# Layer 0 of a hybrid decoder: two feed-forward pairs by token halves and nine by seven products, with zero writes on GpSimd between its convolution additions

## The chip, the cores and the metric

The kernel runs on one core of one Trainium2 chip. The metric is the time of one execution on the device in microseconds (us), as the median of several runs. Where the text says TensorE (PE in the profile), VectorE (DVE), ScalarE (ACT), GpSimd (POOL) and SyncE (SP), it means the five engines of that core. PEld is TensorE's weight load, which overlaps its matmuls.

## The reference

The input is x, 512 tokens of 1024 channels in float32. Two layers follow, and a last RMSNorm. What matters here is layer 0:

```
h = x
# conformer convolution
a = glu(rmsnorm(h) @ w_pw1 + b_pw1)              # 1024 -> 2 x 1024
y = causal depthwise convolution of a, 31 taps, + b_dw
h = h + silu(layernorm(y)) @ w_pw2 + b_pw2       # the "second projection"
# feed-forward
gate, up = split(rmsnorm(h) @ w_up)              # 1024 -> 2 x 2816
h = h + (silu(gate) * up) @ w_down               # 2816 -> 1024
```

Layer 1 is a sliding-window attention over keys and values that are projected from h, and a second feed-forward part of the same shape.

## The kernel before, in words

**Matmuls.** Activations lie transposed: channels on the 128 partitions, tokens along the free dimension. A float32 number is split into two float32r parts, hi and lo, and a product is made of three matmuls, hi x hi, hi x lo and lo x hi (`mm3`, lines 376 to 382). ACT makes hi by a copy and DVE lo by a subtraction (`split_weights`, L294 and L297). The first weight chunks (`NATIVE`, line 133) aren't split and go through L378 in plain float32.

**The stream of weights.** A weight chunk is 128 x 1024 float32, 512 KB. `PLAN` (line 131) lists all chunks in the order in which TensorE uses them. At each use `advance` (lines 299 to 314) issues the loads of chunks up to nine ahead on SP's queue and splits up to three ahead.

**The feed-forward part of layer 0.** The 2816 hidden channels make 11 pairs of 256. `HALVES0` says how they are done.

- Pairs 0 to 3 are done by token halves. For tokens 0 to 255 each pair takes 96 up matmuls and 48 down matmuls of 256 columns (pair 0's up matmuls are native). For tokens 256 to 511 the activations' hi and lo lie side by side, so a hi weight takes both in one matmul of 512 columns and a lo weight one of 256 (`mm2`, L412 and L413). Their weights are loaded and split once for each half.
- Pairs 4 to 10 are done over all tokens by Strassen and Winograd's scheme: the up product is cut into 2 x 2 blocks and made by seven block products (`SEVEN`, line 56) in place of eight. A block product is 24 matmuls of 256 columns (`product`, line 801). Their down matmuls are 512 columns wide, 48 for a pair. Four of the weight blocks are sums (S1 to S4), four of the activation blocks too (T1 to T4).

The sums of weights are made in DRAM: a copy of one block (`copy_sums`), then a DMA from POOL's queue that adds another block to it (`prepare`, lines 277 to 291, L289). `share` says how many of them are issued at each use of a chunk: 0.45 until the products begin, 0.25 in them. The sums of activations are made by `Rows0.sums` (lines 1284 to 1308) on DVE, and split like weights.

**The order of the work.** The first half of the convolution comes first; then the second projection of the first half (`pw2`), the first half of pairs 0 to 3 (up, then down), and three block products A12 of pairs 4 to 6 (`FIRST`), which need the first half's tokens alone. While TensorE does this, the second half's convolution runs on the other engines. Then come the second projection of the second half, the second half of pairs 0 to 3, the remaining 46 block products, and the down matmuls of pairs 4 to 10.

**The convolution.** Of a channel tile's 31 taps, DVE does one part as multiply-adds (L1009). For the other part ACT multiplies (L1001) and POOL adds (L1002). `Half.background` (from line 1108) is a generator that emits the second half's convolution step by step, then its layer norm: squares, sums over channels on TensorE (L1058), scales (L1064 to L1085), their spread over the partitions by one matmul pair (L1089), and eight rows of z = silu(layernorm(y)), each split in hi and lo (L1101 to L1103, then `split`, L544 and L545). The second projection reads z.

**What sets the order.** Instructions are put in order at compile time: each engine takes what is ready, with the first emitted ahead, and `tc.issue_after(x)` forbids that an instruction be put ahead of x on x's engine. `job(generator, (g, n), ...)` says by which use g of a weight chunk how many steps n of a generator have been emitted (`pace`, lines 337 to 344). At run time each engine works through its own order and waits where an input isn't there.

## Time and profile before

| | |
|---|---|
| median of 3 runs | 1043.42 us (1043.19 to 1044.5) |
| the profiled execution | 1043.27 us |
| its span, first to last instruction | 1041.5 us |
| granted TensorE clock, mean | 0.997 |
| second projection of the second half starts | 243.47 us |
| block products of layer 0 start | 335.2 us |
| last convolution addition of POOL (L1002) ends | 208.7 us |

Positions are microseconds from the start of the span. In the profile a group of instructions is named by line, engine, operation and tiles, written as output<-inputs, with the shape and the number of instructions; behind the bar stand its busy time and the mean duration of one in ns, and behind the second bar the engine's idle time just before, with what ended it. A timeline row begins with the start and the duration in us. A matmul's duration overlaps that of its neighbours, so durations of matmuls can't be added.

### The profile page before, as it was taken

The numbers are of one execution on the slowest core, as the hardware profiler recorded it, in microseconds if no ns is written. First come the engines' busy times: TensorE is split into PE (matmuls) and PEld (weight loads), VectorE is DVE, ScalarE is ACT, GpSimd is POOL, SyncE is SP. The second block draws the span as 40 slices with busy tenths as digits, with TensorE's granted clock in tenths as the row PEclk, the third lists the DMA queues.
The fourth block names the chain that finished last, engine by engine and source line by source line (L and its number), as shares of the span: only waits on it lengthen the run. The fifth ranks groups of instructions, "written<-read, shape, count | busy, mean of one in ns | idle before, by whom it ended". The sixth has DMA issues, their size and how long they took to land.

```text
span 1041.5 us, 17709 instructions
## 1 busy us (share of the span) xinstructions
PE 1031.5 (99%) x6580; PEld 932.6 (90%) x6580; DVE 776.5 (75%) x1202; ACT 613.0 (59%) x1062; POOL 473.2 (45%) x569
## 2 busy tenths in 40 slices
PE   9999999999999999999999999999999999999996
PEld 8888889999988999998888877788989999898995
DVE  3999989978789777673536566678686877868777
ACT  3887798847776556552333565466655556554654
POOL 3999999930535233221214255405442334434134
PEclk9999999999999999999999999999999999999998
DMA  9999747999999988999969766955879988877742
GB/s 356 340 315 207 205 126 204 272 256 275 249 239 262 304 220 284 256 301 244 286 209 254 210 183 183 228 154 152 252 230 312 287 264 264 245 233 222 224 150 81
DMA packets 67282, 248.33 MB, mean 238 GB/s; under 512 B 7579, under 2 KB 13884, under 8 KB 66364
## 3 DMA queue, kind: packets, MB, share of 16 engines
q1 hardware_dynamic: 54236, 200.75, 55.9%
q0 software_dynamic: 12672, 46.14, 24.8%
q8 instruction: 51, 0.84, 0.3%
q10 hardware_dynamic: 288, 0.31, 0.1%
q14 instruction: 35, 0.29, 0.1%
HBM read 241.93 MB, written 97.52 MB: 326 GB/s over the span
## 4 chain that ended last, share of the span: by engine, by line
PE 98%; DMA 0%; DVE 0%; issue 0%; POOLq 0%; SPq 0%; POOL 0%; ACT 0%
PE bank L380 20%; PE bank L382 20%; PE bank L381 20%; PE bank L960 10%; PE bank L902 9%; PE bank L412 4%; PE bank L378 4%; PE bank L413 2%; PE bank L1441 1%; PE bank L1483 1%; PE bank L1470 1%; PE bank L1058 1%; PE bank L1607 1%; PE bank L948 1%; DMA both<-in_lead_dram 0%; PE bank L1562 0%
## 5 line engine op out<-in xcount | busy, mean ns | idle before, releaser
L297 DVE TENSOR_TENSOR wlo<-raw,whi 128x1024 fp32r<-128x1024 f32 x246 | 329.7, 1348 | 136.8 <-ACT whi L294 136.5
L294 ACT CAST whi<-raw 128x1024 fp32r<-128x1024 f32 x246 | 257.1, 1049 | 276.6 <-PE bank L381 194.1
L380 PE MATMUL bank<-quad,whi 128*128 128x256 f32 (+1 forms) x976 | 307.4, 317 | 0.0
L381 PE MATMUL bank<-quad,whi 128*128 128x256 f32 (+1 forms) x976 | 306.6, 315 | 0.0
L382 PE MATMUL bank<-quad,wlo 128*128 128x256 f32 (+1 forms) x976 | 305.7, 315 | 0.0
L380 PEld LDWEIGHTS bank<-quad,whi 128*128 128x128 f32 x976 | 185.5, 191 | 12.8 <-issue 1.6
L381 PEld LDWEIGHTS bank<-quad,whi 128*128 128x128 f32 x976 | 186.0, 191 | 11.9 <-issue 0.5
L382 PEld LDWEIGHTS bank<-quad,wlo 128*128 128x128 f32 x976 | 185.6, 191 | 11.8 <-issue 0.4
L853 POOL TENSOR_TENSOR up<-up 128x512 f32<-128x512 f32 x34 | 62.9, 1851 | 283.6 <-ACT up L850 283.6
L1002 POOL TENSOR_TENSOR pr<-pr,pr 128x256 f32<-128x256 f32 x208 | 155.4, 788 | 2.6 <-ACT pr L1001 2.5
L380 PE MATMUL bank<-rows,whi 128*128 128x256 f32 x488 | 138.0, 283 | 0.0
L381 PE MATMUL bank<-rows,whi 128*128 128x256 f32 x488 | 137.8, 282 | 0.0
L382 PE MATMUL bank<-rows,wlo 128*128 128x256 f32 x488 | 137.8, 282 | 0.0
L1009 DVE SCALAR_TENSOR_TENSOR bank<-apad,wdw,bank 128x256 f32<-128x256 f32 x248 | 112.4, 485 | 3.4
L1001 ACT ACTIVATE pr<-apad,wdw 128x256 f32<-128x256 f32 x208 | 98.3, 502 | 14.9 <-POOL pr L1002 13.1
L960 PE MATMUL bank<-quad,w 128*128 128x256 f32 x448 | 98.7, 380 | 0.0
L960 PEld LDWEIGHTS bank<-quad,w 128*128 128x128 f32 x448 | 84.9, 190 | 11.8 <-DVE bank L1009 0.2
L380 PEld LDWEIGHTS bank<-rows,whi 128*128 128x128 f32 x488 | 93.1, 191 | 0.3
L381 PEld LDWEIGHTS bank<-rows,whi 128*128 128x128 f32 x488 | 93.1, 191 | 0.3
L382 PEld LDWEIGHTS bank<-rows,wlo 128*128 128x128 f32 x488 | 93.0, 191 | 0.0
L491 POOL TENSOR_TENSOR tmp<-tmp,tmp 128x256 f32<-128x256 f32 (+1 forms) x28 | 26.8, 957 | 101.4 <-ACT tmp L487 96.2
L412 PE MATMUL bank<-quad,whi 128*128 128x512 f32 x168 | 59.7, 398 | 0.0
(230 smaller groups left out, 1635.9 us busy)
## 6 DMA issues: line engine op xcount, KB each, us to landing
raw<-in_W_dram SPq DMA_DIRECT2D x170, 512.0 KB, 5.7
raw<-sum SPq DMA_DIRECT2D x88, 512.0 KB, 5.4
sum<-in_W_dram SPq DMA_DIRECT2D x52, 512.0 KB, 6.2
sum<-in_W_dram POOLq DMA_DIRECT2D x44, 512.0 KB, 9.6
sum<-sum POOLq DMA_DIRECT2D x44, 512.0 KB, 8.5
sum<-in_W_dram SPq DMA_DIRECT2D x4, 3584.0 KB, 30.4
w<-in_W_dram SPq DMA_DIRECT2D x14, 512.0 KB, 8.6
sum<-in_W_dram SPq DMA_DIRECT2D x4, 1024.0 KB, 30.3
```

The costliest lines, as they stand in the source:

```text
L294: on_act = nc.scalar.copy(hi, src).ins
L297: latest[:] = [on_act, lo_engine[0].tensor_sub(lo, src, f32(hi)).ins]
L380: nc.tensor.matmul(out, w[0], x[0], start=start, stop=False, **kw)
L381: nc.tensor.matmul(out, w[0], x[1], start=False, stop=False, **kw)
L382: nc.tensor.matmul(out, w[1], x[0], start=False, stop=stop, **kw)
L412: nc.tensor.matmul(first[2], first[0], first[1], start=start, stop=False)
L853: pool_op(nc.gpsimd.tensor_mul(gate, gate, c[:, m, :, 1, :]))
L902: nc.tensor.matmul(out, x, w[:, ws], start=first and e == 0 and i == 0, stop=e == 1 and i == 2, skip_group_check=True)
L960: mm = nc.tensor.matmul(self.pb[:, w * W2:(w + 1) * W2], w1_of(ct, w, k), x[k] if x else xg[k][:, tok], start=k == 0, stop=k == KT - 1)
L1001: on_act = nc.scalar.mul(pr, a[:, j:j + W2], tap(j))
L1002: on_pool = pool_op(nc.gpsimd.tensor_add(pr, acc, pr))
L1009: on_dve = nc.vector.scalar_tensor_tensor(yt if i == nd - 1 else c, src, tap(i), c if i else self.shift, op0=ALU.mult, op1=ALU.add)
```

## The change

Pairs 0 and 1 are done by token halves, pairs 2 to 10 by seven products. The nine are done in two groups, pairs 2 to 6 and 7 to 10, each with its products and then its down matmuls (`GROUPS0`). All nine have their A12 product made ahead of the second half's second projection. The results wait in one quad and five tiles of their own (`keep`). The background job is paced at each half of such a product.

The sums over channels, the scales' small matmuls and the spread of the second half's layer norm are put behind the matmul that was emitted last (`stamp`). The steps of the jobs get new points, and `share` becomes 0.5 and 0.45. The pool of part 2 has four buffers in place of five, and odd pairs take their gate tile from the quads. After each of POOL's convolution additions of the second half, from the point where its job begins, and after each of its eight multiplications in the second half's down evacuation, POOL writes zeros to a tile of 128 x 64 (`let_go`).

```diff
-HALVES0 = ((0, 4), (4, 11))
-FIRST = (4, 5, 6)
+HALVES0 = ((0, 2), (2, 11))
+GROUPS0 = ((2, 7), (7, 11))
+FIRST = tuple(range(2, 11))
...
-    plan.extend(("up0", *step) for step in part2_products())
-    downs(*HALVES0[1])
+    for group in GROUPS0:
+        plan.extend(("up0", *step) for step in part2_products(group))
+        downs(*group)
...
-EARLY = (0, sum(u[0] == "up0" for u in UNITS), 9)
+EARLY = (0, 6, 9)
...
+    letting = []
+
     def pool_op(op):
         pooled[0] = op.ins
+        return op
+
+    def let_go(op):
+        if letting:
+            with tc.issue_after(op.ins):
+                pool_op(nc.gpsimd.memset(letting[0], 0.0))
         return op
...
-        nc.tensor.matmul(out, w[1], x[0], start=False, stop=stop, **kw)
+        stamp[0] = nc.tensor.matmul(out, w[1], x[0], start=False, stop=stop, **kw).ins
...
-                    pool_op(nc.gpsimd.tensor_mul(t, t, rs_bc))
+                    let_go(pool_op(nc.gpsimd.tensor_mul(t, t, rs_bc)))
...
-    def product(key, block, r, opens, closes=True):
+    def product(key, block, r, opens, between=None):
 
         w = [x.rearrange("p (a k c) -> p a k c", a=2, k=4) for x in get_seven(*key)]
         for which in range(2):
+            if which and between is not None:
+                between()
...
-                            on_pool = pool_op(nc.gpsimd.tensor_add(pr, acc, pr))
+                            on_pool = let_go(pool_op(nc.gpsimd.tensor_add(pr, acc, pr)))
...
                 for n, (_, f) in enumerate(due):
-                    f()
+                    with tc.issue_after(stamp[0]):
+                        f()
                     for _ in range((4, 1)[n]):
                         yield
-                self.scales_a()
+                with tc.issue_after(stamp[0]):
+                    self.scales_a()
                 yield
                 self.scales_b()
                 withheld.clear()
                 yield
                 yield
                 yield
-                self.spread()
+                with tc.issue_after(stamp[0]):
+                    self.spread()
                 yield from self.rows(True)
...
-        job(second, (base, 0), (base + 8, 19), (base + 13, 22), (base + 26, 40), (base + 30, 45), (base + 34, 50), (base + 35, h1.n_steps - early - 3))
+        letting.append(cpool.tile([P, 64], F32, tag="letting", name="letting"))
+        job(second, (base, 0), (base + 8, 19), (base + 13, 22), (base + 27, 39), (base + 33, 43), (base + 34, 44), (base + 35, 44),
+            (base + 36, 46), (base + 37, 48), (base + 38, 49), (base + 40, h1.n_steps - early))
...
-        preparing[0], share[0] = prepare(), 0.45
+        preparing[0], share[0] = prepare(), 0.5
...
-            product(("up0", pair, "A12"), [[x0["ffn0"][4 + k][e][:, HALF[0]] for k in range(4)] for e in range(2)], r, True)
+            product(("up0", pair, "A12"), [[x0["ffn0"][4 + k][e][:, HALF[0]] for k in range(4)] for e in range(2)], r, True, pace)
...
-    job(rows0.sums(), (base + 11, 0), (base + 19, 8), (base + 26, 14), (base + 32, 17))
+    job(rows0.sums(), (base + 10, 0), (base + 14, 8), (base + 18, 12), (base + 23, 14), (base + 27, 17))
     pw2(h1.z, n1)
     ffn_part(0, 0, x0["ffn0"], HALF[1], n1.rms, twin=True)
-    flush()
...
-    share[0] = 1 / 4
+    share[0] = 0.45
+    for group in GROUPS0:
...
+            if pair not in open_pairs:
+                if pair % 2:
+                    c = quads.tile([P, 2, 2, 2, 256], F32, tag="quad", name=uid("up"))
+                else:
+                    c = z0.tile([P, 2, 2, 2, 256], F32, tag="z0", name=uid("up"), bufs=4)
+                open_pairs[pair] = SevenPair("up0", pair, rows0, c, first.get(pair))
+            pace()
+            open_pairs[pair].take(a)
...
```

77 lines of the change are left out of this document (41 added, 36 removed).

## The prediction

> **What bounds the kernel now.** I read the page first: span, busy shares, and the chain of work that ended last.
>
> ```profile
> span 1041.5 us, 17709 instructions
> PE 1031.5 (99%) x6580; PEld 932.6 (90%) x6580; DVE 776.5 (75%) x1202; ACT 613.0 (59%) x1062; POOL 473.2 (45%) x569
> PE 98%; DMA 0%; DVE 0%; issue 0%; POOLq 0%; SPq 0%; POOL 0%; ACT 0%
> ```
>
> TensorE is never without work, and the chain consists of it: the time is the sum of matmul spacings, and no other engine makes it wait. So a change gains what it takes off TensorE's list, as long as no wait appears. A busy time of one matmul overlaps its neighbour's, so the price of one is taken from stretches that hold one form: length divided by count. The next view gives the busy time of each engine in such stretches (us and number of matmuls under PE; the last two columns are the share of time that the DMA engines were busy, and GB/s).
>
> ```profile
> core 0: us, PE busy (x) PEld busy (x) DVE busy (x) ACT busy (x) POOL busy (x), PEclk, DMA share, GB/s
> 234.74:243.47 8.73, 8.73 (x72) 8.49 (x71) 8.70 (x18) 6.09 (x11) 0.00 (x0) 1.00 1.05 268
> 266.81:312.69 45.88, 45.88 (x264) 40.01 (x263) 37.60 (x43) 33.23 (x58) 18.94 (x18) 1.00 0.96 258
> 312.69:335.21 22.52, 22.52 (x129) 19.59 (x128) 22.32 (x28) 14.13 (x21) 10.18 (x10) 1.00 0.93 270
> 335.22:464.08 128.86, 128.86 (x1082) 128.86 (x1080) 95.90 (x110) 72.34 (x94) 37.45 (x28) 1.00 0.92 267
> 477.90:543.18 65.28, 65.28 (x289) 54.05 (x288) 25.86 (x26) 20.34 (x26) 12.65 (x17) 1.00 0.88 258
> ```
>
> They are: the three early products (72 matmuls); the second half's up matmuls of four pairs; its down matmuls; 45 products; and 288 down matmuls over all 512 tokens. An edge can add one or two to a count. The clock is 1.00 throughout.
>
> **What leaves TensorE.** A pair done by token halves costs:
> - first half: 96 up and 48 down matmuls of 256 columns at 8.73/72 = 0.1213 us: 11.64 + 5.82 us;
> - second half: (45.88 - 0.6 for the six norm matmuls in it)/4 = 11.32 and 22.52/4 = 5.63 us.
>
> Together 34.41 us. By seven products it costs one early product of 8.73/3 = 2.91, six of 128.86/45 = 2.864, and 48 wide down matmuls of 65.28/288 = 0.2267: 2.91 + 17.18 + 10.88 = 30.97 us. Two pairs gain 2 x 3.44 = 6.88. Four more pairs have their A12 product moved to the early place, 0.05 each dearer: **6.7 us** net. Without a new wait the profiled execution (1043.27 us, its span plus 1.8; the median shown is 1043.42) becomes **1036.6 us**.
>
> **Weights.** A moved pair needs 9 chunks in place of 2 x 6, so six splits (ACT L294, DVE L297) go, beside TensorE's work: nothing gained directly. Eight more sums are copied and added by DMA, eight more additions issued on POOL's queue: hidden unless the DMA engines run short (a rival).
>
> **The first new wait: the second projection.** It needs z of the second half's convolution, which DVE, POOL and ACT make while TensorE works on the first half. Two pairs' up and down work (2 x 17.46 us) goes from ahead of it, six products (17.46 us) come, so TensorE arrives 17.46 us earlier than at 243.47: at 226.0. What z went through before:
>
> ```profile
> 172.17:234.73 62.56, 62.56 (x510) 61.93 (x509) 53.62 (x76) 40.16 (x68) 42.78 (x47) 1.00 0.96 264
> 215.92 0.87 DVE L1009 SCALAR_TENSOR_TENSOR y<-apad,wdw,bank 128x256 f32<-128x256 f32 x2
> 216.54 2.42 POOL L1013 TENSOR_TENSOR y<-y,pr 128x256 f32<-128x256 f32 x2 [7.84 <-DVE y L1009]
> 234.28 1.02 PE L1089 MATMUL bank<-tmp,ones_m 128*128 128x512 f32 x2
> 240.99 0.76 DVE L545 TENSOR_TENSOR quad<-tmp,quad 128x256 fp32r<-128x256 f32 x2
> 251.83 0.75 DVE L545 TENSOR_TENSOR quad<-tmp,quad 128x256 fp32r<-128x256 f32 x2
> ```
>
> The first row is the first half's split matmuls: 480 x 0.1213 = 58.2 us, and 4.3 for norms (0.6) and the convolution's sums and spread. The taps ended at 216.8, y at 218.9, the spread of the scales ran at 234.28, the first two rows of z stood at 241.8, two us ahead of need, and the last two at 252.6 (their chunk was due at 252.2). The order of the tail is now tied to the products: sums after the first half of the seventh, spread after the first half of the ninth.
>
> Do the taps end in time? The costs in 157.7:216.7, and of zero writes at the start:
>
> ```profile
> L297 DVE TENSOR_TENSOR wlo<-raw,whi 128x1024 fp32r<-128x1024 f32 x17 | 26.5, 1567 | 2.1 <-ACT whi L294 2.1
> L662 DVE TENSOR_TENSOR bank<-bank,tmp 128x512 f32<-128x512 f32 x4 | 2.7, 687 | 0.0
> L1002 POOL TENSOR_TENSOR pr<-pr,pr 128x256 f32<-128x256 f32 x66 | 57.4, 918 | 2.6 <-ACT pr L1001 2.5
> L937 POOL MEMSET apad<- 128x30 f32 x8 | 0.6, 121 | 0.0
> L462 POOL MEMSET ones_m<- 128x128 f32 x1 | 0.2, 205 | 0.0
> 206.84 1.86 POOL L1002 TENSOR_TENSOR pr<-pr,pr 128x256 f32<-128x256 f32 x2
> 186.51 3.08 POOL L1002 TENSOR_TENSOR pr<-pr,pr 128x256 f32<-128x256 f32 x4
> 187.24 3.45 DVE L297 TENSOR_TENSOR wlo<-raw,whi 128x1024 fp32r<-128x1024 f32 x1
> 214.79 1.22 DVE L297 TENSOR_TENSOR wlo<-raw,whi 128x1024 fp32r<-128x1024 f32 x1
> ```
>
> A split takes 1.22 us when POOL is quiet, and took 3.45 behind POOL's run of four additions. The 17 took 26.5 us, so 26.5 - 17 x 1.22 = 5.8 us were waiting. POOL's additions suffer too: 66 from 137 to 209 took 0.918 us on average. The zero writes, one after each addition, break the runs: DVE gains 0 to 5.8 us; I take half. Up to the end of the taps DVE further loses 1.5 splits (2.4 us), six of the twelve gate operations (4.1) and 2.1 idle, and gets eight down evacuations (5.5, which came later before). So they end 3.1 to 8.9 us earlier, at 208 to 214. POOL gets 66 writes of 64 columns, which no row shows. Rows of 30 and 128 columns bound them at 0.07 (0.6/8, overlapped) and 0.2 us; I take 0.12 between: 8 us, less 2.6 idle and about 2 for splits that no longer block it. Its run ended at 208.7, so now near 212 (bounds 209 to 217). y is then whole at about 214, sums can start at 215. TensorE reaches their place after 172.2 + 0.6 + 11.64 (pair 1 up) + 2 x 5.82 (down) = 196.1, and 6.5 x 2.91 more: 215.0, just in time.
>
> What stays is the tail. The spread can't run before 196.1 + 8.5 x 2.91 + 3.0 for the sums' own matmuls (of the 4.3) = 223.8, and after it TensorE has only the last half product (1.46 us) left. A row of z costs, by the rows of those operations:
>
> ```profile
> L1101 DVE TENSOR_TENSOR tmp<-y,bank 128x256 f32<-128x256 f32 x8 | 3.3, 415 | 0.0
> L1102 DVE TENSOR_TENSOR tmp<-tmp,bank 128x256 f32<-128x256 f32 x8 | 3.3, 416 | 0.0
> L1103 ACT ACTIVATE tmp<-tmp,prm 128x256 f32<-128x256 f32 x8 | 4.5, 597 | 0.0
> L544 ACT CAST quad<-tmp 128x256 fp32r<-128x256 f32 x8 | 3.0, 401 | 0.0
> L545 DVE TENSOR_TENSOR quad<-tmp,quad 128x256 fp32r<-128x256 f32 x8 | 3.1, 420 | 0.0
> ```
>
> That is 2.25 us in sequence: z's first row stands at 224.3 + 2.25 + 0.3 between engines = 226.8 at the earliest, one split later at 228, against 225.7 needed: 1.1 to 2.3 us late. Then a row costs DVE 1.25 and half a split (0.61) in each 1.46 us of TensorE (12 matmuls), or 1.6 as the rows ran before (241.8 to 252.6, two at each end): 0.15 to 0.4 behind per row, 1 to 2.8 over seven. I take **3.0 us** of wait (bounds 0 and 5).
>
> **The second new wait: Winograd's sums.** T1 to T3 must be made in two pairs' time in place of four. Before, DVE was full there:
>
> ```profile
> 301.50:341.00 39.50, 39.50 (x242) 35.10 (x241) 39.30 (x49) 24.54 (x36) 18.76 (x18) 1.00 0.92 253
> L1295 DVE TENSOR_TENSOR plain<-plain,t 128x1024 f32<-128x1024 f32 x1 | 2.3, 2318 | 0.0
> 339.93 0.68 DVE L830 TENSOR_TENSOR up<-bank,quad 128x512 f32<-128x512 f32 x1
> 340.93 0.28 PE L380 MATMUL bank<-rows,whi 128*128 128x256 f32 x1
> ```
>
> The first product's evacuation ended at 340.6 and S2, which adds into the same bank, began at 340.93: 0.3 us to spare. In the new order about 12 splits, two gate evacuations, the down evacuations and three of the four T's must fit in 33 us: by the shares of the old stretch 34, so 0 to 3 us late. T4 is put behind the first products, and the first up tile must wait for plain1's buffer, free after T3's split; both end near 288, S2 starts at 291. I take **0.3 us**.
>
> **The sum:** 1043.27 - 6.7 + 3.0 + 0.3 = 1039.9, say **1039.8 us**.
>
> **Rivals.** *All is hidden:* z comes as early as TensorE, since the taps lose all of POOL's 5.8 us and splits stay out of the tail: **1036.6**. For it: no wait anywhere in the profile before. Against: the two pinned places, 1.46 us apart from need.
>
> *The zeros do not pay (the change does not do what it says):* POOL becomes the last. At 0.2 us per write its run ends at 217, y at 218.7, sums 3.4 us after TensorE is there; the tail follows whole: **1043.2**, no change. It decides when the last y addition ends after 215.7. The Trainium skill (SBUF — State Buffer, "SBUF: two separate sides") says that the port pair shared by DVE and GpSimd goes to whichever starts first, for its whole instruction. By that, what DVE wins between two additions POOL loses, 1.2 us for each split, which is this rival; the 3.45 us row and the additions of 0.918 against 0.73 alone agree with the lock.
>
> *Slower: the DMA engines run short* in the products of pairs 2 to 10.
>
> ```profile
> q1 hardware_dynamic: 54236, 200.75, 55.9%
> q0 software_dynamic: 12672, 46.14, 24.8%
> raw<-sum SPq DMA_DIRECT2D x88, 512.0 KB, 5.4
> sum<-sum POOLq DMA_DIRECT2D x44, 512.0 KB, 8.5
> ```
>
> Queue 1's MB takes 0.559 x 1041.5/200.75 = 2.90 us of all engines, an adding one of queue 0 5.60. So 512 KB loaded or copied is 1.52 us, added 2.93. Before, a product with 0.25 sums needed 1.52 + 0.25 x 4.45 = 2.63 in 2.864 us: 0.92, as its stretch shows. With 0.45 it needs 3.52. Copies join after some 12 products, so 18 products lag 12 us, the ten down chunks of 5.44 us each win it back, and 24 more lag 16 us. Loads are issued nine chunks (25.8 us) ahead, less 5.4 to 8.5 to land: 17 us. If DMA is 10% dearer than this, the lag is 24 us and TensorE waits 7 to 8: **1047.5**. It decides at a lag of 17 us. Against it: 16 is still under 17, and wide down matmuls drain it.
>
> **Chances.** Forecast 0.43 (1037.5 to 1042), all hidden 0.20, zeros do not pay 0.20, DMA short 0.14, something else late 0.03. A measurement of this kernel tells about 0.2% from no change, 2.1 us. Faster by over that: 0.20 + 0.9 x 0.43 + 0.01 = 0.60; within: 0.04 + 0.18 = 0.22; slower: 0.18. The range 1036.0 to 1046.0 leaves out most of the DMA case and little else.
>
> **What would show it.** Right: 240 splits, six products more ahead of the second projection, which starts near 229 after a gap of about 3 us in TensorE, the only one over 1 us; splits in 157:215 near 1.4 us. Wrong: no gap there (then 1036.6), POOL's last y after 216, idle TensorE behind raw loads in the second group of products, or S2 of pair 2 waiting for DVE.

## The result and the profile after

The kernel after takes **1066.62 us** (median of four, 1064.86 to 1068.63) against 1043.31 us of before beside it: 1.0222 of before, 95% interval 1.0205 to 1.0238. The forecast was 1039.8. The profiled execution took 1068.63 us with a span of 1066.6. Line numbers of after are 10 to 22 higher than before's: L392 to L394 are the split matmuls, L424 and L425 those of the second half, L304 and L307 the splits, L1018 POOL's convolution additions, L1025 DVE's taps, L1029 the last addition of y, L276 the zero write, L519 the power of the norm on POOL, L541 its spread.

The page of after: span, busy shares, chain.

```profile
span 1066.6 us, 17672 instructions
PE 1035.5 (97%) x6532; PEld 934.7 (88%) x6532; DVE 780.4 (73%) x1206; ACT 610.1 (57%) x1056; POOL 493.3 (46%) x647
PE 88%; DVE 4%; ACT 3%; issue 2%; POOL 2%; DMA 0%; POOLq 0%; DVEq 0%; ACTq 0%
```

There are 48 matmuls fewer, and still TensorE counts 4 us more as busy: many ran slower. It is 88% of the chain in place of 98. The busy times by stage of after follow (columns as in the prediction); one stage of before, the second projection, stands below them.

```profile
172.21:198.72 26.51, 15.22 (x108) 14.35 (x106) 19.50 (x24) 13.23 (x25) 23.25 (x45) 0.86 0.96 247
198.72:213.24 14.52, 14.38 (x97) 14.09 (x98) 9.08 (x14) 7.84 (x15) 6.72 (x11) 0.79 0.45 118
213.24:246.73 33.49, 29.80 (x237) 28.56 (x235) 24.59 (x40) 20.66 (x35) 21.64 (x32) 0.98 0.82 223
246.73:272.42 25.69, 25.69 (x192) 25.69 (x193) 20.03 (x36) 16.30 (x29) 3.94 (x5) 0.89 0.85 200
284.38:299.36 14.98, 11.53 (x66) 9.84 (x65) 11.52 (x14) 12.70 (x25) 6.02 (x5) 1.00 0.84 211
299.36:314.11 14.75, 13.03 (x64) 11.08 (x65) 14.48 (x18) 7.98 (x13) 5.94 (x8) 0.88 0.90 250
314.11:403.74 89.63, 88.73 (x721) 87.55 (x720) 72.19 (x86) 49.81 (x66) 33.23 (x34) 1.00 0.97 277
```

```profile
243.76:266.80 23.04, 23.04 (x194) 23.04 (x193) 18.81 (x31) 15.33 (x27) 3.92 (x5) 1.00 0.79 241
```

The table sets each stage of after beside the list of matmuls at the prices of before.

| stage of after | list | measured | more |
|---|---|---|---|
| first half, pair 1 up (11.64 and the norm's 0.6) | 12.2 | 26.5 | 14.3 |
| first half, downs | 11.6 | 14.5 | 2.9 |
| nine A12 products (26.2, and 3.0 of the convolution's) | 29.2 | 33.5 | 4.3 |
| second projection | 23.0 | 25.7 | 2.7 |
| second half, pair 1 up | 11.4 | 15.0 | 3.6 |
| second half, downs | 11.3 | 14.8 | 3.5 |
| 29 products and 24 wide down matmuls (29 x 2.864 + 24 x 0.2267) | 88.5 | 89.6 | 1.1 |

Together 32.4 us, against 31.8 between the span and the forecast without waits (1041.5 - 6.7 = 1034.8). Two thirds lie in the first half, the rest behind it. What TensorE waited for is the next view of after (us in total, times, longest).

```profile
PE bank L392 <- ACT quad L556: 10.3, 2, 8.2
PE bank L424 <- DVE quad L665: 5.2, 2, 3.5
PE bank L541 <- ACT tmp L527: 3.1, 1, 3.1
PE bank L1105 <- ACT tmp L1101: 1.7, 1, 1.7
PE bank L392 <- DVE up L844: 0.9, 1, 0.9
```

These rows add up to 21.2 us; before had none of them. They are, from above: hidden values of the first half and the first row of z (8.2 and 2.1); the second half's hidden values; the first half's norm; the spread of z's scales; S2. No row names a load.

**The first gap.** The chain of waits of after from 176 to 199 us (start, length, what):

```profile
176.77 2.38 POOL pr L1018 x2
179.23 0.70 POOL sq L1060
180.08 0.16 POOL letting L276
...
180.92 0.15 POOL letting L276
181.18 1.88 POOL sum L299 x2
183.23 0.69 POOL rs L519
184.24 0.39 ACT tmp L527
...
188.21 5.07 DVE wlo L307
194.20 0.68 DVE tmp L671
197.45 0.60 DVE bank L674
```

The norm's mean square stood ready at 176.6. Its power (L519) came 6.6 us later, behind two additions, one more, zero writes that have no addition left between them, and two DMA issues: a queue works in order. TensorE waited for the spread from 181.6 to 184.7. While it stood, no weight buffer came free: ACT waited 5.3 us for a matmul before it could make the next hi, DVE 6.1 us for that hi, so no split was made either. At 188.2 a split had to be made ahead of the gates (L671, L674), and it took 5.07 us in place of 1.2. DVE and POOL of after in that stretch:

```profile
188.21 5.07 DVE L307 TENSOR_TENSOR wlo<-raw,whi 128x1024 fp32r<-128x1024 f32 x1
190.14 0.98 POOL L1018 TENSOR_TENSOR pr<-pr,pr 128x256 f32<-128x256 f32 x1
190.81 0.40 POOL L276 MEMSET letting<- 128x64 f32 x1
190.91 0.97 POOL L1018 TENSOR_TENSOR pr<-pr,pr 128x256 f32<-128x256 f32 x1
191.66 1.07 POOL L299 DMA_DIRECT2D sum<-in_W_dram  x1
192.23 1.63 POOL L1018 TENSOR_TENSOR pr<-pr,pr 128x256 f32<-128x256 f32 x1
```

The zero writes stand between the additions, as the change wants it, and DVE waits all the same. It came to its turn at POOL's next DMA issue: the addition behind that is the one that was held up (1.63).

**The slow matmuls.** The same busy view of the four stretches in which TensorE worked at a granted clock of 0.50 (the last column but two), each behind a gap:

```profile
184.68:187.67 2.99, 2.99 (x12) 2.81 (x13) 2.08 (x2) 2.99 (x6) 1.85 (x6) 0.50 1.01 185
198.72:204.74 6.02, 5.88 (x26) 5.59 (x27) 1.90 (x4) 0.59 (x1) 0.00 (x0) 0.50 0.35 135
246.73:252.53 5.80, 5.80 (x27) 5.80 (x28) 5.72 (x17) 5.08 (x11) 0.00 (x0) 0.50 1.03 231
300.31:303.73 3.42, 3.42 (x12) 2.86 (x12) 3.42 (x5) 1.06 (x1) 1.43 (x1) 0.50 0.97 264
```

TensorE hardly stands still in them (18.1 of 18.2 us are busy). In the third row 27 matmuls take 5.80 us, 0.215 each, where the prediction's price at a clock of 1.00 is 0.1213. So a gap costs more than its length: of these 18.2 us at half the clock, half, 9.1, is lost. With the 21.2 us of waits that makes 30.3 of the 31.8.

### The profile page after: what moved, and what is told of

It is laid out like the page before. It is cut to its first block, busy times and chain, and to the rows that moved or that the text cites. A ratio compares the mean times of both kernels' runs of the same rounds, so it can differ in the third digit from the quotient of the medians.

```text
span 1066.6 us, 17672 instructions
## 1 busy us (share of the span) xinstructions
PE 1035.5 (97%) x6532; PEld 934.7 (88%) x6532; DVE 780.4 (73%) x1206; ACT 610.1 (57%) x1056; POOL 493.3 (46%) x647
## 4 chain that ended last, share of the span: by engine, by line
PE 88%; DVE 4%; ACT 3%; issue 2%; POOL 2%; DMA 0%; POOLq 0%; DVEq 0%; ACTq 0%
PE bank L392 20%; PE bank L393 20%; PE bank L394 20%; PE bank L916 9%; PE bank L976 8%; PE bank L424 2%; DVE bank L1025 1%; PE bank L1471 1%; PE bank L1513 1%; PE bank L1500 1%; PE bank L425 1%; POOL pr L1018 1%; DVE wlo L307 1%; ACT pr L1017 1%; PE bank L1074 1%
## 5 line engine op out<-in xcount | busy, mean ns | idle before, releaser
L307 DVE TENSOR_TENSOR wlo<-raw,whi 128x1024 fp32r<-128x1024 f32 x240 | 319.3, 1337 | 153.4 <-ACT whi L304 153.1
L304 ACT CAST whi<-raw 128x1024 fp32r<-128x1024 f32 x240 | 250.8, 1048 | 294.3 <-PE bank L393 206.6
L392 PE MATMUL bank<-quad,whi 128*128 128x256 f32 (+1 forms) x976 | 313.2, 324 | 10.3 <-ACT quad L556 10.3
L393 PE MATMUL bank<-quad,whi 128*128 128x256 f32 (+1 forms) x976 | 312.8, 321 | 0.1
L394 PE MATMUL bank<-quad,wlo 128*128 128x256 f32 (+1 forms) x976 | 310.3, 321 | 0.0
L867 POOL TENSOR_TENSOR up<-up 128x512 f32<-128x512 f32 x38 | 71.0, 1869 | 333.5 <-ACT up L864 333.5
L392 PEld LDWEIGHTS bank<-quad,whi 128*128 128x128 f32 x976 | 188.3, 194 | 25.4 <-ACT quad L556 11.5
L393 PEld LDWEIGHTS bank<-quad,whi 128*128 128x128 f32 x976 | 188.5, 193 | 13.3 <-DVE quad L557 0.4
L394 PEld LDWEIGHTS bank<-quad,wlo 128*128 128x128 f32 x976 | 187.8, 193 | 13.0 <-issue 0.4
L1018 POOL TENSOR_TENSOR pr<-pr,pr 128x256 f32<-128x256 f32 x208 | 160.7, 821 | 9.9 <-ACT pr L1017 9.9
L392 PE MATMUL bank<-rows,whi 128*128 128x256 f32 x536 | 151.6, 283 | 0.9 <-DVE up L844 0.9
L394 PE MATMUL bank<-rows,wlo 128*128 128x256 f32 x536 | 151.4, 282 | 0.0
L393 PE MATMUL bank<-rows,whi 128*128 128x256 f32 x536 | 151.4, 282 | 0.0
L1025 DVE SCALAR_TENSOR_TENSOR bank<-apad,wdw,bank 128x256 f32<-128x256 f32 x248 | 112.5, 485 | 3.5
L392 PEld LDWEIGHTS bank<-rows,whi 128*128 128x128 f32 x536 | 102.1, 191 | 1.4 <-issue 1.1
L393 PEld LDWEIGHTS bank<-rows,whi 128*128 128x128 f32 x536 | 102.1, 191 | 0.3
L394 PEld LDWEIGHTS bank<-rows,wlo 128*128 128x128 f32 x536 | 102.1, 190 | 0.0
L916 PE MATMUL bank<-wlo,fhi 128*128 128x512 f32 x140 | 55.2, 394 | 0.0
```

Of the source, the lines that this page charges most:

```text
L304: on_act = nc.scalar.copy(hi, src).ins
L307: latest[:] = [on_act, lo_engine[0].tensor_sub(lo, src, f32(hi)).ins]
L392: nc.tensor.matmul(out, w[0], x[0], start=start, stop=False, **kw)
L393: nc.tensor.matmul(out, w[0], x[1], start=False, stop=False, **kw)
L394: stamp[0] = nc.tensor.matmul(out, w[1], x[0], start=False, stop=stop, **kw).ins
L867: pool_op(nc.gpsimd.tensor_mul(gate, gate, c[:, m, :, 1, :]))
```

## The experiments

The ratios are to runs of before on the same chip, each with its 95% interval. "Scale" below is before at 1043.3 us. The theory at the start was *cover*: two pairs leave the gates no work to lie behind. The rival: the zero writes hold POOL and DVE.

### Without and with the zero writes alone (e1, e2)

e1 is after without the line that switches the writes on; e2 is before with `let_go` and that line.

```diff
-        letting.append(cpool.tile([P, 64], F32, tag="letting", name="letting"))
```

> The kernel after, without the zero writes on POOL; nothing else is changed. Theory (cover): with two pairs, the first half's down matmuls follow at once on the up matmuls whose gates they need, and TensorE waits for the gate work (8.4 us at 190 in the kernel after); the zero writes only add to the delay of the power of the norm on POOL (3.2 us at 181). So the gap near 190 stays at 6 to 10 us, the one near 181 falls below 1.5, and the time is 1060 to 1066 us. Rival (zeros): the writes are the cause of both gaps, since POOL's queue stands in front of the norm and DVE's split gets no turn: both gaps fall below 2 us each and the time is 1050 to 1054. If DVE is held without the writes as much as with them, the longest split in the stretch of the gap still takes 3.5 us or more.

> The kernel before, with the zero writes behind each convolution addition of POOL and each of the eight multiplications of the second half, and nothing else of the change. Theory (cover): four pairs leave TensorE work enough, so no gap opens: 1042 to 1045 us; the split in DVE behind POOL's run of additions is as long as before (3.45 us) or longer, so the writes free nothing. Rival (zeros): the writes delay POOL's power and DVE's splits enough to make TensorE wait: 1047 or more. If the writes do what they are for, the longest split in the convolution's stretch is under 2 us and the mean of the splits there falls from 1.57 to about 1.3.

e1 took 1.0204 (1.0188 to 1.0219), not to be told from after; e2, in the order of before, 1.0066 (1.005 to 1.0083), 6.9 us slower than before. e1's gap at 181 fell from 3.1 to 1.4 us, the one for the gates stayed at 8.6: cover, not the zeros, as the theory had it. But e2 came out as the rival said. Two waits of TensorE in it, the first for a split of 5.62 us, the second for the norm's spread:

```profile
PE bank L390 <- DVE wlo L305: 4.4, 1, 4.4
PE bank L537 <- ACT tmp L523: 1.8, 1, 1.8
```

Groups of splits up to the end of the taps, from before, after, e1 and e2, one row each:

```profile
L297 DVE TENSOR_TENSOR wlo<-raw,whi 128x1024 fp32r<-128x1024 f32 x18 | 28.1, 1572 | 2.1 <-ACT whi L294 2.1
```

```profile
L307 DVE TENSOR_TENSOR wlo<-raw,whi 128x1024 fp32r<-128x1024 f32 x17 | 28.7, 1697 | 13.4 <-ACT whi L304 13.4
```

```profile
L307 DVE TENSOR_TENSOR wlo<-raw,whi 128x1024 fp32r<-128x1024 f32 x18 | 35.1, 1960 | 7.5 <-ACT whi L304 7.5
```

```profile
L305 DVE TENSOR_TENSOR wlo<-raw,whi 128x1024 fp32r<-128x1024 f32 x18 | 38.0, 2122 | 3.3 <-ACT whi L302 3.3
```

In the order of before the writes free nothing: the mean split is 1.57 us without them and 2.12 with them (e2). In the order of after it is 1.96 without them (e1) and 1.70 with them, and the time is the same. The writes also change the compiled order of all engines, and the longest splits come and go with the order: e1 has one of 5.50 us without any write.

### TensorE kept at work in the gaps (e3, e13)

```diff
+    def fill(n):
+        b = bank()
+        with tc.issue_after(stamp[0]):
+            for _ in range(n):
+                stamp[0] = nc.tensor.matmul(b[:, 0:P], ones_m, ones_m, start=True, stop=True).ins
...
+                        if pending:
+                            fill(27)
...
+        if not twin:
+            fill(68)
```

> The kernel after, with TensorE kept at work in its first two gaps by matmuls whose result nobody reads: 27 of 128 columns (2.9 us) ahead of the norm's spread near 181, 68 (7.4 us) between the first half's up and down matmuls. Theory (clock): what follows a gap runs at about half the clock for 3 to 5 us (0.213 us for a matmul of 0.120), and that is a loss beside the gap itself. The first down matmul starts as before near 198.7 (within 1 us), but those behind it run at 0.12 us: 3 to 6 us faster than the kernel after, 1061 to 1064 us. Rival (no clock effect; the slow stretches are waits for weights or evacuations): no gain, or a loss of up to 3 us where the fill is longer than the gap: 1066 to 1070.

> The kernel after with the two fills at half their number, 13 and 33 matmuls, since one of 128 columns in float32 took 0.22 us and not 0.11: 2.9 and 7.3 us. Theory (clock): the granted clock stays at 1.00 through both fills and the first half's down matmuls take 11.6 to 12 us as in e3_filled, not 14.5; the fills end about when the gates are there, so the second projection starts 3 to 6 us earlier than in the kernel after: 1.016 to 1.019 of before, 1060 to 1063.5 us on the scale of before at 1043.3. Rival (a fill only holds a place in the row): 1.021 to 1.024.

e3: 1.0285 (1.027 to 1.0301), slower than either side expected. A fill matmul took twice what was reckoned, so the second fill ended about 9 us after the hidden values were there. e13, with half as many: 1.0197 (1.0182 to 1.0213), just above the range of the theory; its interval overlaps that of after, so it is the stages that tell. In both the downs behind the fill ran at full clock; the row of e13:

```profile
195.83:207.42 11.59, 11.59 (x99) 11.59 (x98) 9.37 (x15) 7.59 (x15) 9.02 (x17) 1.00 0.92 213
```

11.59 us against 14.52 in after, with the same matmuls: 2.9 us of that stage are clock alone. In e13 the second projection starts at 241.8, 5 us ahead of after's 246.7, as expected; but the 29 products and 24 wide down matmuls of the table's last row take 92.3 us and not 89.6, with 2.0 us of wait ahead of S2, so half of it is given back.

### Products between up and down (e4)

```diff
+        if part == 0:
+            plan.extend(("up0", pair, "A12") for pair in FIRST[:4])
         downs(*HALVES0[0])
         if part == 0:
-            plan.extend(("up0", pair, "A12") for pair in FIRST)
+            plan.extend(("up0", pair, "A12") for pair in FIRST[4:])
```

> The kernel after, with four of the nine early products put between the first half's up and down matmuls, in place of behind the downs; the amount of work is the same. Theory (cover): 11.6 us of products cover the gate work, so the gap near 190 goes with the slow matmuls behind it (8.4 + 3 to 4 us): 1053 to 1057 us; the gaps at the norm near 181, ahead of the second projection and in the second half stay. Rival (zeros or POOL as the bound): the gap only moves to the second projection, since the convolution's taps are what is late, and the time stays within 3 us of the kernel after: 1063 to 1068.

1.0213 (1.0185 to 1.024): a miss for the theory. The 8.2 us gap fell to 0.5, but a gap of 3.2 us opened in the downs, 3.0 us ahead of the second projection stayed, which started at 242.0, and S2 waited 2.4. The split that the downs waited for (DVE's timeline of e4):

```profile
207.00 5.81 DVE L309 TENSOR_TENSOR wlo<-raw,whi 128x1024 fp32r<-128x1024 f32 x1
```

So cover alone was too narrow a theory. The next one: *DVE's fixed row of splits, gates and taps, held by POOL's additions, sets the pace of the first half*; less work on TensorE only lets the waits show.

### POOL's additions left out (e8), downs by pair (e7), three pairs (e6)

```diff
-                            on_pool = let_go(pool_op(nc.gpsimd.tensor_add(pr, acc, pr)))
+                            on_pool = on_act if self.hf else pool_op(nc.gpsimd.tensor_add(pr, acc, pr))
```

> The kernel after, with POOL's additions in the second half's convolution left out, and the zero writes behind them (ACT's products are still made; the convolution then lacks their sum). Theory (POOL's additions hold DVE, DVE's order is what the first half waits for): the splits of the stretch take 1.2 to 1.8 us each, the gaps near 181 and 190 come to under 4 us together, the last tap ends before 220, the second projection starts at 227 to 234 in place of 246.7, and the time is 1046 to 1055 us. Rival (two pairs give the gates no cover, whatever POOL does): the gap near 190 stays at 5 us or more, and the time is above 1057.

1.0169 (1.0153 to 1.0184), which is the rival's time; the second projection started at 241.6, not at 227 to 234. All splits up to the end of the taps took 1.2 to 1.7 us and the norm's gap was gone, but TensorE's waits in e8 still have the gates in the first row:

```profile
PE bank L392 <- ACT quad L556: 7.1, 2, 5.0
```

5.0 of the 8.2 us stay with POOL's additions gone: that part is missing cover (with a third pair, in e18 below, it is gone). The rest (3.2) and the norm's 3.1 are POOL's; of the norm's, 1.7 go with the zero writes alone (e1). Neither theory was right alone.

```diff
         steps = [(g, kp) for g in range(2) for kp in range(lo, hi)]
+        if (lo, hi) == HALVES0[0]:
+            steps.sort(key=lambda s: s[1])
+        for g, kp in steps:
+            plan.append(("down", 0, kp, g))
...
-        for g in range(2):
-            if twin:
-                banks = [bank().rearrange("p (a s) -> p a s", a=2) for _ in range(4)]
-                for kp in range(lo, hi):
+        for kp in range(lo, hi):
+            for g in range(2):
+                if kp == lo:
+                    fulls[g] = [bank().rearrange("p (a s) -> p a s", a=2) for _ in range(n_banks)]
```

The banks of both column groups are held for that.

> The kernel after, with the down matmuls of the two pairs by halves ordered by pair, both column groups of pair 0 ahead of those of pair 1, so that pair 1's gate work has 5.6 us of matmuls to lie behind, not 2.8. Theory (gate cover in the second half): the gaps at 295 and 306 (3.6 and 1.9 us, and the slow matmuls behind them) go: pair 1's up matmuls and the downs of the second half take 23 to 26 us together, not 29.7; the first half gains 0 to 3 us, since DVE sets its pace; in all 1058 to 1062 us on the scale of before at 1043.3. Rival (DVE is the bound in the second half, whatever order TensorE has): the wait turns up at the products instead (S1 or S2 behind T1 or T2), and the time stays at 1064 to 1068.

1.0223 (1.0204 to 1.0241): no gain, the rival. The first gap of the second half is a wait for pair 0's own hidden values, which no order of the downs covers. DVE of after in front of them (L665), with a sum T1 (L1317) and a split that took 2.99 us:

```profile
294.04 1.66 DVE L1317 TENSOR_TENSOR t<-plain,plain 128x1024 f32<-128x1024 f32 x1
295.62 2.99 DVE L307 TENSOR_TENSOR wlo<-raw,whi 128x1024 fp32r<-128x1024 f32 x1
298.54 0.68 DVE L665 TENSOR_TENSOR quad<-tmp,quad 128x512 fp32r<-128x512 f32 x1
```

```diff
-HALVES0 = ((0, 2), (2, 11))
-GROUPS0 = ((2, 7), (7, 11))
-FIRST = tuple(range(2, 11))
+HALVES0 = ((0, 3), (3, 11))
+GROUPS0 = ((3, 7), (7, 11))
+FIRST = tuple(range(3, 11))
...
-        letting.append(cpool.tile([P, 64], F32, tag="letting", name="letting"))
```

The zero writes are left out here and in every kernel that builds on this one (e10, e12, e15 to e18); the due places of the background job and of the sums are shifted by one to four uses of a chunk.

> The kernel after, with three pairs by token halves and eight by seven products (groups of pairs 3 to 6 and 7 to 10), all eight A12 products early, job points in between those of before and of after, and no zero writes. TensorE's list is 3.4 us shorter than before, and ahead of the second projection it has some 83 us of work from the end of the native matmuls of the first projection on, against 86 before and 69 after. Theory (the two-pair order leaves the other engines too little time in both halves): no gap over 1 us ahead of the second projection, little in the second half, so 0.996 to 1.000 of before, 1039 to 1043.5 us on the scale of before at 1043.3. Rival (DVE is full in the second half already with four pairs, and every pair less costs a wait): 3 to 6 us of gaps between 290 and 335, 1043 to 1047.

1.0074 (1.0057 to 1.0091), slower than either side expected. With a third pair the two gaps of the second half are gone (11.35, 11.27 and 16.85 us for pairs 1 and 2 up and three downs, the list's price). S2 waits 2.3 us. In the first half 6.0 us of waits are left, 3.5 of them for splits, with this row of DVE among the causes (e6):

```profile
201.39 5.36 DVE L307 TENSOR_TENSOR wlo<-raw,whi 128x1024 fp32r<-128x1024 f32 x1
```

### DVE against POOL by itself (e5, e9)

> The kernel after, with twelve small races put behind its end, which its result does not need (so its total time is not compared). In each, DVE makes the lo part of a weight chunk (128 x 1024, two operands in SBUF, as in every split) right after the first of POOL's additions of 128 x 256: three times beside one addition, then beside eight in a row, beside eight with a zero write of 128 x 64 between each two, and with one of 128 x 512. Theory (the write frees DVE): 1.2 us alone, 5 to 6.5 behind the bare row, under 2.5 with the narrow write. Rival (a narrow write is too short to let go, or does not let go at all): 5 us or more with the narrow write; the wide one then tells which, by under 2.5 us if only the width was lacking.

> As the first races behind the end of the kernel after (total time not compared), but with POOL's twelve further additions in two chains that take turns, as the convolution's are, so that none waits for the one before it; in the first races each waited for the one before. Four cases, three times each: turns without writes, turns with a zero write of 128 x 64 after each addition, with one of 128 x 512, and two of one chain and then two of the other. Theory (additions that overlap keep the port): DVE's split takes 4 us or more in the first case and with the narrow write, where the next addition begins before the one before has ended; 1.2 to 2.6 us with two and two, where every second addition waits. The wide write shows whether any write lets go: under 2.5 us if so. Rival (the port goes to DVE after one addition in any order): 1.8 us in all four, and the long splits in the kernel have another cause.

```diff
+            if width:
+                with tc.issue_after(last):
+                    last = nc.gpsimd.memset(zeros[:, 0:width], 0.0).ins
+            with tc.issue_after(last):
+                last = nc.gpsimd.tensor_add(t, seed, t).ins
```

One split each: in e5 beside one addition, and in e9 beside two chains in turns without a write, with one of 64 columns, with one of 512.

```profile
1096.47 1.22 DVE L1754 TENSOR_TENSOR wlo<-raw,whi 128x1024 fp32r<-128x1024 f32 x1
```

```profile
1122.02 1.78 DVE L1743 TENSOR_TENSOR wlo<-raw,whi 128x1024 fp32r<-128x1024 f32 x1
1135.65 1.78 DVE L1744 TENSOR_TENSOR wlo<-raw,whi 128x1024 fp32r<-128x1024 f32 x1
1150.13 1.22 DVE L1745 TENSOR_TENSOR wlo<-raw,whi 128x1024 fp32r<-128x1024 f32 x1
```

A miss for the theory: in these races DVE waits for one addition at most (0.56 us) whether or not a narrow write stands there, and with the wide write not at all. The fourth case of e9, two and two of one chain, gave 1.78 us as well. Neither race reproduces a wait of 4 to 6 us. What makes POOL keep its turn in the kernel is not settled here.

### POOL's additions two and two (e10, e11)

e10 is e6 with this edit, e11 is after with it, without the zero writes:

```diff
+                    late = self.hf and (i + e) % 2 and i < nd - 1
-                    while pi * nd < n_pool * (i + 1):
+                    while not late and pi * nd < n_pool * (i + 1):
...
-                            on_pool = let_go(pool_op(nc.gpsimd.tensor_add(pr, acc, pr)))
+                            with tc.issue_after(row[0]) if self.hf and row[0] else nullcontext():
+                                on_pool = pool_op(nc.gpsimd.tensor_add(pr, acc, pr))
+                            row[0] = on_pool.ins
```

> The run with three pairs (e6_three), with POOL's additions of the second half's convolution put two and two of one channel tile, so that every second addition waits for the one before it; the same additions, no zero writes. Theory (POOL's row of independent additions holds DVE's splits, and these hold TensorE): no split over 3 us between 157 and 217, the gaps ahead of the second projection fall from 6.6 us to under 2, and the time falls by 6 to 10 us against e6_three: 0.998 to 1.002 of before, 1041 to 1045 us on the scale of before at 1043.3. Rival (three pairs leave too little time whatever the order of POOL): within 3 us of e6_three, 1.005 to 1.009.

> The kernel after without zero writes (e1_no_zeros), with POOL's additions put two and two in the same way. Theory: no split over 3 us, and the first half gains what POOL's hold cost there, as without the additions at all: 5 to 8 us against the kernel after. The gate wait near 190 stays at 4 to 6 us (5.2 were left without any additions), and so does the second half: 1.013 to 1.018 of before, 1057 to 1062 us on the scale of before at 1043.3. Rival (the hold isn't what costs): within 2 us of e1_no_zeros, 1.019 to 1.022.

e10: 1.0047 (1.0029 to 1.0065), e11: 1.0203 (1.0187 to 1.0219). Up to the end of the taps the long splits are gone in both: none over 2.2 us, where e6 had 5.49, 5.36 and 4.54. The group of e10 (mean 2114 ns in e6):

```profile
L307 DVE TENSOR_TENSOR wlo<-raw,whi 128x1024 fp32r<-128x1024 f32 x17 | 25.6, 1516 | 6.6 <-ACT whi L304 6.6
```

With three pairs that brings 2.8 us (1049.7 against 1052.6) where 6 to 10 were expected, which is the rival's "within 3 us": the waits for splits went, but the norm's gap grew from 1.4 to 3.0 us, since POOL's row is as long as it was. With two it brings nothing, the rival again: 6.9 us of gate wait stay.

### The second half's sums on POOL (e14), other orders with three pairs (e12, e15, e16, e17)

```diff
-                    ("T1", t1, nc.vector.tensor_sub, b11, b12), ("T2", b11, nc.vector.tensor_add, b22, t1),
+                    ("T1", t1, nc.gpsimd.tensor_sub, b11, b12), ("T2", b11, nc.gpsimd.tensor_add, b22, t1),
...
-                with tc.issue_after(latest[1]):
-                    f(t, a, b)
+                with tc.issue_after(pooled[0]):
+                    pool_op(f(t, a, b))
```

T3 and T4 go to POOL likewise.

> The kernel after, with the four sums of activations T1 to T4 made by POOL and not by DVE (1.6 to 2.3 us each on DVE). Theory (in the second half DVE's row is what the two pairs' gates wait in: a sum T of 1.59 us stands ahead of pair 0's gate at 294, one of 1.01 ahead of pair 1's at 306.8): the gaps at 295 and 306 fall from 5.5 us together to 1 to 3.5, with some of the slow matmuls behind them: 2 to 5 us faster than the kernel after, 1.017 to 1.020 of before. Rival (POOL's longer sums, and its hold on DVE, come late themselves: S1 or S2 waits for T1 or T2): 1.021 to 1.026.

1.0334 (1.032 to 1.0348), the rival: the waits for the second half's hidden values grew from 5.2 to 10.0 us. POOL stands in the gates' chain too.

e12 is e10 with the held pair's evacuation (the spread of the norm and the gates) one group of matmuls later and S4 ahead of S2:

```diff
-                    if half == 1 and which == 0:
+                    if half == 1 and which == 1:
                         for p in pending:
...
-            names = ["A11", "S1", "S2", "S4", "S3", "A22"]
+            names = ["A11", "S1", "S4", "S2", "S3", "A22"]
...
-                nc.scalar.copy(c12, r)
+                if self.kind == "up0":
+                    nc.vector.tensor_add(c12, r, c12)
```

> The run with three pairs and POOL's additions two and two (e10_three_serial), with two more moves: the gate work of pair 0 in the first half is put behind pair 1's last up chunk, not its third (so the norm's spread is asked for 2.9 us later, and three pairs leave room for it); and in the products S4 stands ahead of S2, so that S2, which adds into the bank that A11's sum is still read from, comes one product later. Theory (each wait goes when the order gives it cover, and the slow matmuls behind it go with it): the gap at 182 (3.2 us) and the one ahead of S2 (2.5 us) fall below 0.5 us each, with about 2 and 1.5 us of slow matmuls: 8 to 9 us less than e10_three_serial, 0.995 to 0.998 of before, 1038 to 1041 us on the scale of before at 1043.3. Rival (DVE has no room with three pairs, the waits only move): 1.001 to 1.005.

1.0079 (1.0066 to 1.0092), slower than the rival: the norm's gap went, 3.6 us of gaps came in its place in the next stages, and the third product still waited 2.3 us. In the trace that product still reads a sum of activations (`rows`), which S4 does not: S4 did not come ahead of it, so this move was not tried.

e15 is e10 with the first half's norm taken earlier:

```diff
-                    if twin and half == 0 and which == 1 or pending and half + which == 0:
+                    if twin and half == 0 and which == 1 or w == 256 and not twin and pair == lo and half + which == 2:
                         rms.step1()
```

e16 is e15 with the two operations that end a down evacuation both on POOL:

```diff
-                    let_go(pool_op(nc.gpsimd.tensor_mul(t, t, rs_bc)))
-                    nc.vector.tensor_add(hm, hm, t)
+                    pool_op(nc.gpsimd.tensor_mul(t, t, rs_bc))
+                    pool_op(nc.gpsimd.tensor_add(hm, hm, t))
```

> The run with three pairs and POOL's additions two and two (e10_three_serial), with one move: the small matmuls of the first half's norm stand right behind pair 0's last up chunk, not behind pair 1's first, so that the power on POOL is asked for 2.9 us earlier and stands ahead of two additions in POOL's row. Theory (the power on POOL is all that the spread near 182 waits for): that gap falls from 3.2 us to 1.5 or less, with most of the 2 us of slow matmuls behind it: 2.5 to 5 us less than e10_three_serial, 1.000 to 1.0025 of before. Rival (the convolution's chain is what is late, and the time saved is waited for at the second projection): 1.0035 to 1.0055.

> As e15_three_norm, and the eight additions into h behind the second half's down matmuls are made by POOL, not by DVE (0.41 us each on DVE), so that DVE comes to the evacuation of A11 sooner. Theory (DVE's row is what S2 waits in): the gap ahead of S2 (2.5 us) falls below 1, with 1.5 us of slow matmuls: 2 to 4 us less than e15_three_norm, 0.997 to 1.0005 of before. Rival (POOL's additions hold DVE there as they did in the convolution): the gap stays, 0 to 4 us more than e15_three_norm.

e15: 1.0043 (1.003 to 1.0055), the gap fell from 3.0 to 1.8 us, and its gain was lost in the downs (0.8 us) and ahead of the convolution's sums (0.9). e16: 1.0015 (1.0006 to 1.0024); the wait ahead of S2 is gone, and there DVE's row was what was late.

e17 is e16 with the first A12 product within pair 1's up, behind its first two chunks:

```diff
             plan.extend(ups(0, pair))
+            if part == 0 and pair == 1:
+                plan.insert(len(plan) - 2, ("up0", FIRST[0], "A12"))
```

> As e16_three_more, with the first of the eight A12 products put in the middle of pair 1's up matmuls of the first half, ahead of the norm's spread, and the sums over channels asked for one half product later; the work is the same. Theory (what is left of the shorter list's gain is lost in single waits without cover): the gaps at 182 (2.0 us) and at 224 (1.1 us) fall below 0.5 us, with a fourth to a third as much again of slow matmuls: 3 to 4.5 us less than e16_three_more, 0.997 to 0.9985 of before, 1040 to 1042 us on the scale of before at 1043.3. Rival (DVE and POOL have no room in the first half, a wait moved is a wait that comes back at the second projection): 1.0005 to 1.002.

1.0026 (1.0017 to 1.0035), the rival and a little above its range: both gaps went, and 2.9 us came back as waits for the gates' lo part (L559) in the downs.

### Three pairs without POOL's additions (e18)

The edit is that of e8, in e16.

> As e16_three_more, with POOL's additions in the second half's convolution left out (ACT's products are still made; the convolution lacks their sum). Theory (POOL's and DVE's work for the second half's convolution is what leaves the first half no room): without it the list of matmuls sets the time. From pair 1's first up matmul to the second projection it is 67.7 us (pairs 1 and 2 up 24.1, downs 17.5, eight products 23.1 and the convolution's own matmuls 3.0), against 73.0 in e16_three_more; the gap at 182 goes; the time is 3 to 5 us below e16_three_more, 0.997 to 0.9985 of before. Rival (the gates of three pairs have too little cover in themselves): 71 us or more from there to the second projection, and 1.000 or more of before.

0.9985 (0.9976 to 0.9995). The stretch from pair 1's first up matmul to the second projection, first of e16, then of e18:

```profile
173.36:246.31 72.95, 69.42 (x554) 67.42 (x554) 60.35 (x91) 48.85 (x85) 50.69 (x54) 1.00 0.94 247
```

```profile
175.33:243.46 68.13, 68.13 (x554) 67.28 (x554) 53.04 (x85) 46.84 (x80) 13.71 (x17) 1.00 0.86 233
```

The same 554 matmuls take 4.8 us less and wait for nothing; 67.7 was the list's price. From that matmul to the end of the span e18 needs 1041.4 - 175.33 = 866.1 us and before 1041.5 - 172.17 = 869.3: 3.2 us for one pair, where the prediction's prices give 3.24 (3.44, less 0.05 for each of four more products made early). So the shorter list is worth what it was priced at, once the other engines have room; shown for one pair, in a kernel that leaves out the additions. Its whole time gains 1.5 us only, since e18 comes to that matmul 3.2 us later than before, with waits of 1.7 us near the start and 1.4 us at 130. No complete kernel here beat before; e16 came nearest.

## Why the prediction was wrong, point by point

**What bounds the kernel now.** Right for before: the list of matmuls sets its time. But the condition "as long as no wait appears" was filled in for two places only.

**What leaves TensorE (-6.7).** Right. 48 matmuls fewer; a pair is worth 3.2 us by e18 against 3.24. **Weights:** 240 splits, as forecast.

**The step that failed: the list of waits.** The sum was -6.7 + 3.0 + 0.3. It took the second projection and Winograd's sums as the only places where TensorE could come early. Ahead of them the chains norm, gate, down stayed as long as they were, and had two pairs' matmuls to lie behind in place of four. No term was given to them: the first half's norm (3.1 us of wait), its hidden values (8.2) and the second half's (5.2). With a third pair the last one is gone (e6). That two pairs lack cover accounts for 5.0 of the 8.2 (e8); the rest and the norm's wait come from POOL's row, which loses them when the additions go, 1.7 of the norm's with the zero writes alone (e1).

**"Do the taps end in time?"** No. Forecast was 208 to 214; the last tap and y's last additions in after:

```profile
230.75 0.87 DVE L1025 SCALAR_TENSOR_TENSOR y<-apad,wdw,bank 128x256 f32<-128x256 f32 x2
231.31 2.42 POOL L1029 TENSOR_TENSOR y<-y,pr 128x256 f32<-128x256 f32 x2 [3.35 <-DVE y L1025]
```

The taps ended at 231.6, y at 233.7. The sum counted DVE's work as if DVE ran without a pause. But taps stand behind splits in its fixed order, a split needs a weight buffer that TensorE has done with, and TensorE stood: the group row of after above has 13.4 us of idle time ahead of splits, where before has 2.1. A wait of TensorE was passed on to the engine that it waited for.

**The zero writes.** The price, 0.12 each, lies between two cases. Between additions they cost next to nothing: four additions of after begin 0.77 us apart with a write between each two (188.59 to 190.91), and before's run of four took 0.77 each (3.08). With no addition left between them they stand 0.21 apart (180.08 to 180.92), and six of them stood ahead of the norm's power. What they bring was wrong: half of 5.8 us was credited to DVE, and no gain shows (mean split 1.70 for 1.57; 2.12 in e2, with 6.9 us of time). The rival "the zeros do not pay" had the sign, but its mechanism, POOL as the last, did not happen: y waited for DVE's tap.

**The wait ahead of the second projection (3.0).** The mechanism, a tail pinned close ahead of need, was right; the size was near, in part by luck: 1.7 and 2.1 us of gaps at 242 and 245, in front of a start at 246.7 and not 229, for the spread and for the first row of z. The other part of the term, rows of z that fall behind by 1 to 2.8 us, did not happen: TensorE is busy all through the second projection. The term lacked the slow matmuls behind the gap, 2.65 us there.

**Winograd's sums (0.3).** 0.9 us.

**DMA short.** Did not happen: DMA was busy at a share of 0.97 in the first group of products, and no matmul or split waited for a load.

**What was missing altogether** is the clock. The gaps bring 18.2 us of matmuls at half the clock, which costs 9.1, and the prediction priced every wait at its length.

## What to carry to other kernels

Where TensorE is solid, list each chain that lies behind it (norm, gates, sums) with its length and the work that covers it, before work is taken off; the cover that shrinks is every chain's, not just the one that the change has in mind. A wait of TensorE is then to be priced with what it holds up in turn, the buffers and splits behind it, and with the matmuls at a lower clock after it. An instruction put into a queue to help another engine is to be tried alone, in the old order, first.

## What the runs showed of the hardware that was not expected

**The granted clock can fall after a short gap.** In e6 a gap of 2.3 us ahead of S2 was followed by this:

```profile
332.55:333.90 1.35, 1.35 (x11) 1.35 (x12) 1.35 (x3) 0.00 (x0) 1.15 (x2) 1.00 1.07 212
333.90:337.20 3.30, 3.30 (x18) 3.30 (x17) 3.30 (x6) 0.43 (x1) 3.30 (x5) 0.50 1.02 377
```

The first 1.35 us run at full clock, then 3.3 us at half: some 1.6 us lost beside the gap. After the 8.2 us gap of after it was 6.0 us. In e10 and e15 the same gap of 2.3 us was followed by 3.4 us at 0.50, too; in e12 it was followed by no fall (the granted clock of 250 to 700 is 1.00 there), and neither was one of 1.9 us in e16; so the length of the gap alone does not decide. The Trainium skill (TensorE: Matmul & The Clock Gate, "Part 1: The HAM clock gate") says that the array drops to half its clock after an idle window of about 3.4 us and comes back after a like time of work. The rows agree with the half and with the return after 3.3 us; here a gap of 2.3 us was enough in e6 and not in e12.

**A waiting DVE operation can be passed over.** By the rule of the Trainium skill that the prediction cites (SBUF — State Buffer, "SBUF: two separate sides") whoever starts first holds the port pair for its whole instruction. The races agree (1.78 = 0.56 + 1.22, a wait for one addition); in the kernel splits of 5 us and more waited behind four to six additions, in after and in e6 until POOL issued a DMA. With the additions two and two no split up to the end of the taps took over 2.2 us in e10 and e11, but e15 and e17, built on e10, have one of 2.62 and one of 4.43. Why the kernel differs from the races stays open.
